# Up projection of a decoder layer in seven block products per pair of row blocks, with half-size weight slices

## Chip, cores, metric

One core of a Trainium2 chip runs the whole layer in one launch. The metric is the device time of that core in microseconds; "before" is the median of 3 runs. TensorE is called PE here, VectorE DVE, ScalarE ACT, GpSimd POOL and SyncE SP. Each engine takes its instructions strictly in the order in which the program wrote them and waits on semaphores that others raise.

## Reference, cut to what matters

```python
mix = jnp.concatenate([attn, gated], axis=-1)
h = h + mix @ w_out                                                    # 1024 x 1024
f = jnp.square(jax.nn.relu(rmsnorm(h, norm2_g) @ w_up)) @ w_down       # 1024 x 4096, 4096 x 1024
h = h + f
gate = jax.nn.sigmoid(rmsnorm(h, gate_norm_g) @ w_gate)                # 1024 x 1024
return h + gate * (p @ w_ple)                                          # then the final rmsnorm
```

There are 2080 tokens (32 of the decoder sample, 2048 of the prompt), float32 throughout. Ahead of this stand the input projection, the dilated attention and the gated mixing; none of that is touched.

## The kernel before, in words

The tail (function `finish`) keeps activations transposed, features on the partitions and tokens along the free axis, in four **groups** of 544, 512, 512 and 512 tokens (`GROUPS`). A float32 product is made of three fast matmuls: every operand is split into a rounded high half and the low remainder, and `mm3` (L1440 to L1448) issues high x high (L1443), high x low (L1444) and low x high (L1445) into one PSUM bank. A matmul's stationary operand is a 128x128 piece of weights, its moving operand up to 512 tokens; group 0 is cut into two halves of 272.

The work is a flat list of jobs J, one after another on PE. `up_job(g, f)` makes row block f of the hidden layer (32 blocks of 128): 8 contraction blocks x 3 matmuls over the tokens, then relu (L1477), square (L1478) and the high copy (L1479) on ACT and the low remainder on DVE (L1480). `down_job(g, f, 2)` takes two row blocks of the hidden layer and adds 8 output blocks, 2 x 3 matmuls each, into `acc` on DVE (L1493). A steady stretch is two up jobs and a down job: 48 + 48 matmuls of 512 columns, called a **pair** below; 16 pairs make a group. The gate jobs of group g-1 and the output projection (`out_job`) of group g+1 are put between the pairs of group g, and the second norm of group g+1 (`norm`, L1407 to L1411) is spread behind its output projection, several pairs before that group begins: `zha/zla` and `zhb/zlb` alternate, so one group's operand is written while the other is read.

Weights come as **slices** of 128x1024: a DMA into one of two raw buffers (L1269), a high copy on ACT (`S.copy`, L1287), a low remainder on POOL or, for every fourth slice, on DVE (L1288). Five slices stand in a ring (`RING = 5`). A slice is written into the queues some steps ahead of its use (`split_one`, at most one per 3 steps of PE time), or, where it has not been by then, right at its first use (`Weights.__getitem__`). Since each queue is in order, what stands ahead of the copy in ACT's queue has to be done before it.

`bg()` runs one piece of the waiting elementwise work (norms, loads, final scaling) at every yield of a job, so those pieces stand between the job's own instructions.

Of the kernel before, what the change touches and what calls it, by code (L numbers as in the profile page):

```python
# [8 lines left out]
F32 = mybir.dt.float32  # L9
F32R = mybir.dt.float32r  # L10
# [4 lines left out]
P = 128  # L15
# [22 lines left out]
WX, WY = 18, (4, 2, 1)  # L38
RING, EXTRA = 5, (9, 7, 6, 5, 4, 3)
# [8 lines left out]
def build(tc, A, stop=9):  # L48
# [12 lines left out]
    with stack:  # L61
# [23 lines left out]
        zero = cp.tile([P, P], F32, name="zero")  # L85
        V.memset(zero, 0.0)
# [1163 lines left out]
        def finish(sa, att, ape):  # L1250
            zt, acc, sq_sum, hid = {}, {}, {}, {}
            work, adds = [], []
# [5 lines left out]

            def w1(nm):
                return wk.tile([P, GM], F32, tag="w1", name=nm, bufs=3)  # L1260


            wraw, wbuf = [], []

            def wload(t, src):
                if t == 0:
                    wraw.append(ape.tile([P, 2, 1024], F32, tag="kh0", name="wraw"))
                raw = wraw[0][:, t % 2]
                nc.sync.dma_start(raw if len(src.shape) == 2 else raw.rearrange("p (a b) -> p a b", a=2), src)  # L1269


            def slot(t):
                if t not in LATE:
                    if t < RING:
                        tag = ("q10", "qd2", "kl0", "raw", "raw")[t]
                        wbuf.append(ape.tile([P, 2, 1024], F32R, tag=tag, name=f"w{t}", bufs=1 + (tag == "raw")))
                    return wbuf[ring_no(t) % RING]
                e = LATE.index(t)
                if e % 2 == 0:
                    b = wk.tile([P, KD, GM], F32R, tag=("zha", "zla", "acca")[e // 2], name=f"w{t}")  # L1280
                    b = b.rearrange("p a b -> p (a b)")[:, :4096].rearrange("p (s a b) -> p s a b", s=2, a=2)
                    wbuf[RING:] = [b[:, 0], b[:, 1]]
                return wbuf[RING + e % 2]

            def wsplit(t):
                w, raw = slot(t), wraw[0][:, t % 2]
                S.copy(w[:, 0], raw)  # L1287
                (V if t % 4 == 3 else G).tensor_sub(w[:, 1], raw, w[:, 0].bitcast(F32))  # L1288
                return w[:, 0], w[:, 1]


            rings = {}

            def ring(tag, i, n):
# [17 lines left out]
            def mix(g):  # L1312
# [9 lines left out]
                for a in range(3 if g else 0):  # L1322
                    load()
# [5 lines left out]
                for a in range(4):  # L1329
# [8 lines left out]
                    if g and a == 2:  # L1338
# [8 lines left out]
                        for _ in range(8):  # L1347
                            yield
# [465 lines left out]
```

## Time and profile before

| what | value |
|---|---|
| runs | 2918.13 us median of 3 (2916.2 to 2918.51) |
| profiled execution | 2915.15 us, span 2913.3 us, mean granted clock 0.976 |
| PE busy | 2798.0 us of the span (96%) |
| DVE, ACT, POOL busy | 1515.2, 1299.9, 1265.0 us |
| the four groups | from about 1180 us to the end |

The span is the time from the first to the last instruction; the execution's own time is 1.85 us longer. A PE that is busy is not a PE at its peak, since matmuls overlap: what one costs is read from the distance between the starts of neighbours.

### The profile page before, as it was taken

How to read it: one execution, taken by the hardware profiler on the slowest of the kernel's cores; microseconds unless marked ns; L12 is line 12 of the kernel's file. 1: busy time of each engine (PE TensorE's matmuls, PEld its weight loads, DVE VectorE, ACT ScalarE, POOL GpSimd, SP SyncE). 2: the span in 40 equal slices, each digit the busy share in tenths (PEclk: the TensorE clock that was granted, in tenths of full speed). 3: DMA queues.
4: the chain of work that ended last, by engine and by line, in shares of the span. 5: the costliest groups of instructions: out<-in, count | busy, mean ns of one | idle time of the engine just before them, and what ended most of it. 6: DMA issues, size and time to landing. Idle time of an engine off the chain costs nothing.

```text
span 2913.3 us, 42298 instructions
## 1 busy us (share of the span) xinstructions
PE 2798.0 (96%) x15712; PEld 2399.5 (82%) x15712; DVE 1515.2 (52%) x2947; ACT 1299.9 (45%) x2363; POOL 1265.0 (43%) x899
## 2 busy tenths in 40 slices
PE   8999998989998998999999999999999999999997
PEld 8877775668888798899999798888888888888887
DVE  6686246655544457644445455446534455534347
ACT  4222453347877774533334433334433434443343
POOL 2568344534768664532222423334333334433332
PEclk9999999979999999999999999999999999999999
DMA  6668675556765774232222232423233323333232
GB/s 183 205 231 297 196 236 174 150 145 194 214 199 171 228 227 157 77 101 87 88 87 94 77 132 95 163 91 101 87 123 129 131 88 101 105 110 123 98 105 72
DMA packets 218478, 413.34 MB, mean 142 GB/s; under 512 B 19552, under 2 KB 87680, under 8 KB 218272
## 3 DMA queue, kind: packets, MB, share of 16 engines
q1 hardware_dynamic: 215584, 406.45, 43.3%
q10 hardware_dynamic: 2688, 4.20, 0.4%
q8 instruction: 124, 2.03, 0.3%
q14 instruction: 82, 0.67, 0.1%
HBM read 342.61 MB, written 67.96 MB: 141 GB/s over the span
## 4 chain that ended last, share of the span: by engine, by line
PE 57%; DVE 2%; ACT 1%; issue 0%; POOL 0%; POOLq 0%; ACTq 0%; DVEq 0%
PE u L1445 8%; PE u L1443 8%; PE u L1444 8%; PE d L1443 8%; PE d L1444 8%; PE d L1445 8%; PE g L1445 2%; PE g L1444 2%; PE g L1443 2%; DVE ss L1367 1%; PE b L1443 1%; PE b L1445 1%; PE b L1444 1%; DVE zf L1407 0%; ACT sq L1362 0%
## 5 line engine op out<-in xcount | busy, mean ns | idle before, releaser
L1288 POOL TENSOR_TENSOR w<-wraw,w 128x1024 fp32r<-128x1024 f32 x228 | 558.8, 2453 | 992.4 <-ACT w L1287 950.7
L1287 ACT CAST w<-wraw 128x1024 fp32r<-128x1024 f32 x304 | 316.5, 1045 | 348.9 <-PE d L1444 258.9
L1443 PE MATMUL d<-ring,w 128*128 128x512 f32 (+2 forms) x1312 | 457.6, 349 | 0.9 <-ACT ring L1479 0.9
L1443 PE MATMUL u<-zh,w 128*128 128x512 f32 (+1 forms) x1280 | 453.2, 354 | 3.0 <-ACT sq L1362 1.8
L1493 DVE TENSOR_TENSOR acc<-acc,d 128x512 f32<-128x512 f32 (+2 forms) x640 | 360.6, 577 | 182.0 <-PE d L1445 181.2
L1444 PE MATMUL d<-ring,w 128*128 128x512 f32 (+2 forms) x1312 | 454.8, 347 | 0.3 <-DVE ring L1480 0.3
L1445 PE MATMUL d<-ring,w 128*128 128x512 f32 (+2 forms) x1312 | 454.5, 346 | 0.0
L1444 PE MATMUL u<-zl,w 128*128 128x512 f32 (+1 forms) x1280 | 449.5, 351 | 2.6 <-POOL zl L1411 1.8
L1445 PE MATMUL u<-zh,w 128*128 128x512 f32 (+1 forms) x1280 | 451.5, 353 | 0.0
L1480 DVE TENSOR_TENSOR ring<-r,ring 128x512 fp32r<-128x512 f32 (+1 forms) x160 | 113.2, 708 | 533.3 <-ACT ring L1479 533.3
L1443 PEld LDWEIGHTS d<-ring,w 128*128 128x128 f32 x1312 | 247.7, 189 | 32.8 <-ACT ring L1479 1.1
L1445 PEld LDWEIGHTS d<-ring,w 128*128 128x128 f32 x1312 | 246.9, 188 | 33.1
L1444 PEld LDWEIGHTS u<-zl,w 128*128 128x128 f32 x1280 | 241.9, 189 | 38.0 <-POOL zl L1411 2.3
L1444 PEld LDWEIGHTS d<-ring,w 128*128 128x128 f32 x1312 | 247.3, 188 | 31.3 <-DVE ring L1480 0.5
L1443 PEld LDWEIGHTS u<-zh,w 128*128 128x128 f32 x1280 | 241.5, 189 | 37.1 <-ACT sq L1362 2.0
L1445 PEld LDWEIGHTS u<-zh,w 128*128 128x128 f32 x1280 | 241.6, 189 | 32.7
L1477 ACT ACTIVATE r<-u 128x512 f32<-128x512 f32 (+1 forms) x160 | 82.6, 516 | 287.3 <-PE u L1445 287.3
L1136 POOL TENSOR_TENSOR fl<-fr,fh 128x512 fp32r<-128x512 f32 (+1 forms) x120 | 128.4, 1075 | 134.2 <-ACT fh L1135 112.9
L306 PE MATMUL f<-xh,wh 128*128 128x512 f32 (+1 forms) x480 | 174.5, 363 | 11.2 <-ACT wh L173 5.6
L958 DVE CUSTOM_DVE_ANT_0 sm<-s,mask 128x256 f32<-128x256 f32 (+1 forms) x384 | 122.3, 363 | 108.5 <-ACT pe L968 38.0
L307 PE MATMUL f<-xl,wh 128*128 128x512 f32 (+1 forms) x480 | 172.1, 359 | 2.4 <-DVE xl L203 2.3
L308 PE MATMUL f<-xh,wl 128*128 128x512 f32 (+1 forms) x480 | 172.3, 359 | 0.4 <-DVE wl L174 0.4
(279 smaller groups left out, 5699.0 us busy)
## 6 DMA issues: line engine op xcount, KB each, us to landing
wraw<-w_up SPq DMA_DIRECT2D x128, 512.0 KB
wraw<-w_down SPq DMA_DIRECT2D x128, 512.0 KB
xr<-xT SPq DMA_DIRECT2D x72, 256.0 KB
sr<-cache_v SPq DMA_DIRECT2D x32, 512.0 KB
wraw<-w_gate SPq DMA_DIRECT2D x32, 512.0 KB
fr<-g_d SPq DMA_DIRECT2D x24, 512.0 KB
wr<-w_in SPq DMA_DIRECT2D x40, 256.0 KB
o_d<-stg SPq DMA_DIRECT2D x32, 264.0 KB
```

The source lines that it names most:

```text
L306: T.matmul(p, wh[:, k, ws], h[:, o:o + w], start=st, stop=False)
L307: T.matmul(p, wh[:, k, ws], l[:, o:o + w], start=False, stop=False)
L308: T.matmul(p, wl[:, k, ws], h[:, o:o + w], start=False, stop=sp)
L958: V.tensor_tensor_reduce(sm[:, c], sp[:, c], mask[:, 256 * d + (256 - P * nk if d < 2 else 0):256 * d + (256 if d < 2 else P)], scale=1.0, ...
L1136: G.tensor_sub(l, raw, h.bitcast(F32))
L1287: S.copy(w[:, 0], raw)
L1288: (V if t % 4 == 3 else G).tensor_sub(w[:, 1], raw, w[:, 0].bitcast(F32))
L1443: T.matmul(p, wh, zh, start=(x == 0), stop=False)
L1444: T.matmul(p, wh, zl, start=False, stop=False)
L1445: T.matmul(p, wl, zh, start=False, stop=(x == n - 1))
L1480: V.tensor_sub(hl[:, c], r, hh[:, c].bitcast(F32))
L1493: V.tensor_add(acc[g][:, d, c], acc[g][:, d, c], p)
```

## The change

For two row blocks of the up projection (f, f+1), the two halves of the contraction (4 of 8 blocks each) and the two halves of the tokens, the 2x2 block product is made from **seven** block products instead of eight (Winograd's form of Strassen's scheme). A product is 4 contraction blocks x 3 matmuls over half a group's tokens (256 or 272): 84 matmuls per pair where there were 48 of 512 columns (96 of 272 in group 0). Around them:

- The weight operands are half slices of 128x512. Three of the seven are halves of the weights, four are sums or differences, made on POOL (L1807) ahead of the split. Every up slice's low half is made on POOL, and of the others two in three. `RING = 8` half slices; six raw places instead of two whole ones.
- The token operands are seven blocks in high and low form (`zc`), one buffer for all groups, made by `blocks(g)`: per contraction block two scalings, four subtractions and two of the low remainders on DVE, four high copies on ACT and two remainders on POOL. `blocks(g+1)` stands behind group g's last up job, between its last two down jobs.
- The products are put together by seven DVE additions of half a group (L1583 to L1597) and one ACT copy (L1581); relu, square, copy and low remainder then run per row block.
- Gate jobs work on half a group, so gate weights are read and split twice per group.

```diff
-RING, EXTRA = 5, (9, 7, 6, 5, 4, 3)
+RING = 8
...
             def up_job(g, f):
                 def run(ws):
...
+                    def prod(x, y):
+                        w = ws[x]
+                        p = ps7[x] = bank(f"u{g}_{f}_{x}", m)
+                        for k in range(4):
+                            kk = slice(P * k, P * k + P)
+                            T.matmul(p, w[0][:, kk], zh[y][:, k, :], start=(k == 0), stop=False)
+                            T.matmul(p, w[0][:, kk], zl[y][:, k, :], start=False, stop=False)
+                            T.matmul(p, w[1][:, kk], zh[y][:, k, :], start=False, stop=(k == 3))
+                            steps[0] += 3 * m / 2400
+                            if k == 1:
+                                yield
+                        use(1)
+                        yield
...
+                    yield from prod(0, 5)
+                    yield from prod(1, 3)
+                    yield from prod(2, 0)
+                    S.copy(U1, ps7[2])
+                    yield from prod(3, 6)
+                    V.tensor_add(U2, U1, ps7[3])
+                    yield from prod(4, 4)
+                    V.tensor_add(U3, U2, ps7[4])
+                    V.tensor_add(U2, U2, ps7[1])
+                    r, t = two(f"r{g}_{f}")
+                    V.tensor_add(r[1], U3, ps7[1])
+                    V.tensor_add(r[0], U3, ps7[0])
+                    for x, c in [(t, slice(0, n))] if t is not None else zip(r, cs):
+                        S.activation(x, x, AF.Relu)
+                        hidden(x, 1, c)
+                    yield from prod(5, 1)
+                    r, t = two(f"q{g}_{f}")
+                    V.tensor_add(r[0], U1, ps7[5])
+                    yield from prod(6, 2)
+                    V.tensor_add(r[1], U2, ps7[6])
+                    for x, c in [(t, slice(0, n))] if t is not None else zip(r, cs):
+                        S.activation(x, x, AF.Relu)
+                        hidden(x, 0, c)
...
+            def make_low():
+                t = low[0]
+                h, o, e, end = sl[t]
+                w = got[t]
+                (G if o or end is False or t % 3 else V).tensor_sub(w[:, 1], place(h), w[:, 0].bitcast(F32))
...
+            def make():
+                if low[0] is not None:
+                    make_low()
+                if not can_make():
+                    return
...
+                if o:
+                    G.tensor_tensor(place(h), place(o[0]), place(o[1]), op=o[2])
+                w = got[t] = slot(t)
+                S.copy(w[:, 0], place(h))
...
+                    t = made[0]
+                    if steps[0] >= last_made[0] + 1.4:
+                        if low[0] is not None or (can_make() and steps[0] >= born[sl[t][0]] + 4):
+                            make()
```

Three places of the built program show how the queues move. First, ACT's queue over one steady pair of group 1. L1809 is the high copy of a weight slice (L1287 before), L1591 and L1599 the relus of the two row blocks, L1567 and L1568 their square and copy, L1581 the copy of product 2. Before, row blocks 24 and 25:

```order
L1477 ACTIVATE r1_24_0_18654<-u1_24_0_18627 128x512
L1478 ACTIVATE r1_24_0_18654<-r1_24_0_18654 128x512
L1479 CAST ring0_12135<-r1_24_0_18654 128x512
L1287 CAST w0_11289<-wraw_11197 128x1024
L1477 ACTIVATE r1_25_0_18687<-u1_25_0_18659 128x512
L1478 ACTIVATE r1_25_0_18687<-r1_25_0_18687 128x512
L1479 CAST ring0_12135<-r1_25_0_18687 128x512
```

and of the change, row blocks 24 and 25 as one pair:

```order
L1581 COPY ring3_12065<-u1_24_2_19939 128x256
L1809 CAST w4_11596<-wraw_11195 128x512
L1591 ACTIVATE r1_24_19988<-r1_24_19988 128x512
L1567 ACTIVATE r1_24_19988<-r1_24_19988 128x512
L1568 CAST ring0_12062<-r1_24_19988 128x512
L1809 CAST w6_11664<-wraw_11195 128x512 x2
L1599 ACTIVATE q1_24_20012<-q1_24_20012 128x512
L1567 ACTIVATE q1_24_20012<-q1_24_20012 128x512
L1568 CAST ring0_12062<-q1_24_20012 128x512
L1809 CAST w0_11289<-wraw_11195 128x512
L1809 CAST w0_11289<-wraw2_11530 128x512
```

The weight copies among the relus were those of up 26 and 27, whose turn on PE comes after the next down job. Now the two copies behind the first relu chain are those of product 6 of this same pair and of the coming down job's first row block (both go to ring tile w6), and the down job's second slice stands behind the second relu chain.

Second, PE over the same stretch, with the semaphores waited for. Before, where up 24 ends and up 25 begins (w2 is its slice, zh21 and zl21 the token operand):

```order
L1444 MATMUL u1_24_0_18627<-zl21_12404,w1_11361 128x512
L1445 MATMUL u1_24_0_18627<-zh21_12403,w1_11361 128x512
L1443 MATMUL u1_25_0_18659<-zh21_12403,w2_11611 128x512 [waits DVE_49,Activation_49]
L1444 MATMUL u1_25_0_18659<-zl21_12404,w2_11611 128x512
L1445 MATMUL u1_25_0_18659<-zh21_12403,w2_11611 128x512
```

and of the change, where product 5 ends and product 6 begins, and where the down job begins (w6 and w0 are ring tiles of two slices each, ring0 to ring2 the hidden layer's high and low parts):

```order
L1559 MATMUL u1_24_5_19998<-zc_first_11505,w4_11596 128x256
L1557 MATMUL u1_24_6_20016<-zc_first_11505,w6_11664 128x256 [waits Activation_49]
L1558 MATMUL u1_24_6_20016<-zc_first_11505,w6_11664 128x256
L1559 MATMUL u1_24_6_20016<-zc_first_11505,w6_11664 128x256 [waits Pool_49]
...
L1517 MATMUL d1_22_0_0_20039<-ring1_12063,w6_11664 128x512 [waits DVE_49,Activation_49]
L1518 MATMUL d1_22_0_0_20039<-ring2_12064,w6_11664 128x512
L1519 MATMUL d1_22_0_0_20039<-ring1_12063,w6_11664 128x512 [waits Pool_49]
L1517 MATMUL d1_22_0_0_20039<-ring0_12062,w0_11289 128x512 [waits Activation_49]
L1518 MATMUL d1_22_0_0_20039<-ring1_12063,w0_11289 128x512
L1519 MATMUL d1_22_0_0_20039<-ring0_12062,w0_11289 128x512 [waits DVE_49]
```

Before, the wait for a slice stands at the head of a job of 24 matmuls. Now product 6 waits at its first matmul for the high half (Activation) and at its third for the low half (Pool), and the down job's two slices are waited for in the same way at its first, third, fourth and sixth matmul.

Third, POOL around the step from group 1 to group 2. Before, the low remainders of the second norm (L1411) among weight slices, behind the twelfth pair of group 1:

```order
L1288 TENSOR_TENSOR w1_11361<-wraw_11197,w1_11361 128x1024
L1288 TENSOR_TENSOR w2_11611<-wraw_11197,w2_11611 128x1024
L1411 TENSOR_TENSOR zl22_19127<-zf22_0_0_19128,zh22_19126 128x512
L1411 TENSOR_TENSOR zl22_19127<-zf22_2_0_19157,zh22_19126 128x512
L1411 TENSOR_TENSOR zl22_19127<-zf22_4_0_19183,zh22_19126 128x512
L1288 TENSOR_TENSOR w4_11782<-wraw_11197,w4_11782 128x1024
L1411 TENSOR_TENSOR zl22_19127<-zf22_6_0_19210,zh22_19126 128x512
L1288 TENSOR_TENSOR w0_11289<-wraw_11197,w0_11289 128x1024
```

and of the change, between the last two down jobs of group 1 (L1439 is the low remainder of a token block, L1782 that of a weight slice):

```order
L1782 TENSOR_TENSOR w0_11289<-wraw2_11530,w0_11289 128x512 x2
L1439 TENSOR_TENSOR zc_first_11505<-wraw2_11530,zc_first_11505 128x2x256
L1439 TENSOR_TENSOR zc_first_11505<-w1b_11531,zc_first_11505 128x2x256
L1439 TENSOR_TENSOR zc_first_11505<-ring3_12065,zc_first_11505 128x2x256 x2
L1439 TENSOR_TENSOR zc_first_11505<-wraw2_11530,zc_first_11505 128x2x256
L1439 TENSOR_TENSOR zc_first_11505<-w1b_11531,zc_first_11505 128x2x256
L1439 TENSOR_TENSOR zc_first_11505<-ring3_12065,zc_first_11505 128x2x256 x2
L1782 TENSOR_TENSOR w2_11480<-wraw_11195,w2_11480 128x512
L1782 TENSOR_TENSOR w4_11596<-wraw_11195,w4_11596 128x512
```

All eight token remainders now stand in one run, behind the first two or three slices of the last-but-one down job and ahead of its fourth (the L1782 row on w2) and of everything the last down job needs.

## Rows read from the trace of the kernel before

**Rows 1.** The page's busy line: busy us, share of span, xinstructions.

```profile
PE 2798.0 (96%) x15712; PEld 2399.5 (82%) x15712; DVE 1515.2 (52%) x2947; ACT 1299.9 (45%) x2363; POOL 1265.0 (43%) x899
```

**Rows 2.** The page's chain that ended last, share of the span by engine.

```profile
PE 57%; DVE 2%; ACT 1%; issue 0%; POOL 0%; POOLq 0%; ACTq 0%; DVEq 0%
```

**Rows 3.** A stage of group 2: busy us by engine, clock, DMA.

```profile
core 0: us, PE busy (x) PEld busy (x) DVE busy (x) ACT busy (x) POOL busy (x), PEclk, DMA share, GB/s
2030.00:2430.00 400.00, 400.00 (x1742) 325.02 (x1742) 192.66 (x248) 156.88 (x223) 146.45 (x64) 1.00 0.34 112
```

**Rows 4.** Waits: waiter, awaited, total us, times, longest.

```profile
POOL w L1288 <- ACT w L1287: 950.7, 198, 12.3
ACT w L1287 <- PE d L1444: 258.9, 41, 9.3
```

**Rows 5.** Timeline of PE: start us, us; pieces of 512, 272, 256 columns.

```profile
2000.09 0.40 PE L1443 MATMUL d<-ring,w 128*128 128x512 f32 x1
...
2011.88 0.40 PE L1443 MATMUL u<-zh,w 128*128 128x512 f32 x1
...
1500.41 0.29 PE L1445 MATMUL u<-zh,w 128*128 128x272 f32 x1
...
1502.67 0.30 PE L1445 MATMUL u<-zh,w 128*128 128x272 f32 x1
...
2869.73 0.28 PE L1443 MATMUL g<-zh,w 128*128 128x256 f32 x1
...
2879.94 0.28 PE L1443 MATMUL g<-zh,w 128*128 128x256 f32 x1
```

**Rows 6.** Timeline: a row block's last matmul and its relu.

```profile
1501.16 0.29 PE L1445 MATMUL u<-zh,w 128*128 128x272 f32 x1
...
1501.49 0.40 ACT L1477 ACTIVATE r<-u 128x272 f32<-128x272 f32 x1 [1.70 <-PE u L1445]
```

**Rows 7.** Tile d: duration ns min/median/max, starts, forms.

```profile
L1493 DVE TENSOR_TENSOR acc<-acc,d x640: 407/676/690, 1217.5 to 2856.2; 128x512 f32<-128x512 f32 x92, 128x272 f32<-128x272 f32 x64, 128x256 f32<-128x256 f32 x4
```

**Rows 8.** Groups by line and form: xcount, busy us, mean ns.

```profile
L1493 DVE TENSOR_TENSOR acc<-acc,d 128x272 f32<-128x272 f32 x256 | 108.2, 435 | 55.1 <-PE d L1445 55.0
...
L1136 POOL TENSOR_TENSOR fl<-fr,fh 128x512 fp32r<-128x512 f32 x72 | 91.9, 1281 | 78.8 <-ACT fh L1135 66.7 <-PE o L999 6.0 <-DMA re<-o_d 4.9
...
L1478 ACT ACTIVATE r<-r 128x512 f32<-128x512 f32 x96 | 60.7, 632 | 3.1
...
L1479 ACT CAST ring<-r 128x512 fp32r<-128x512 f32 x96 | 59.6, 620 | 3.1
...
L1477 ACT ACTIVATE r<-u 128x512 f32<-128x512 f32 x96 | 57.2, 596 | 209.5 <-PE u L1445 209.5
...
L1407 DVE SCALAR_TENSOR_TENSOR zf<-acc,gains,rb 128x512 f32<-128x512 f32 x40 | 48.5, 1212 | 3.0 <-ACT rb L127 3.0
...
L1478 ACT ACTIVATE r<-r 128x272 f32<-128x272 f32 x64 | 27.6, 432 | 2.0
```

**Rows 9.** Windows of 5 us in the last stretch (columns as in rows 3).

```profile
2835.00:2840.00 5.00, 3.92 (x20) 3.95 (x21) 2.60 (x6) 2.76 (x5) 0.48 (x1) 0.66 0.34 120
```

**Rows 10.** Timeline of PE in that stretch.

```profile
2833.96 0.28 PE L1445 MATMUL d<-ring,w 128*128 128x256 f32 x1
...
2836.08 0.85 PE L97 MATMUL rc<-ones,ss 128*128 128x1 f32 x4 [1.85 <-DVE ss L1367]
...
2837.16 0.41 PE L1444 MATMUL d<-ring,w 128*128 128x256 f32 x1
...
2839.50 0.35 PE L1443 MATMUL d<-ring,w 128*128 128x256 f32 x1
```

**Rows 11.** Timeline: a DVE remainder beside POOL's, and one alone.

```profile
2017.87 2.50 POOL L1288 TENSOR_TENSOR w<-wraw,w 128x1024 fp32r<-128x1024 f32 x1 [5.97 <-ACT w L1287]
...
2019.63 1.29 DVE L1480 TENSOR_TENSOR ring<-r,ring 128x512 fp32r<-128x512 f32 x1 [1.53 <-ACT ring L1479]
...
2025.08 0.69 DVE L1480 TENSOR_TENSOR ring<-r,ring 128x512 fp32r<-128x512 f32 x1 [4.15 <-ACT ring L1479]
```

More of the change, by code (lines that the diff above doesn't have):

```diff
@@ L1272, in slot @@
-            def slot(t):
[L1273 to L1294, printed above, removed]
+                more()
+                turn[0] += 1
+                return scratch[turn[0] % 2]
+            wbuf, places, extra = [], [], []
+            def more():
+                if not extra:
+                    assert mixed
+                    t = ape.tile([P, SEQ], F32, tag="raw", name="wraw2", bufs=2)
+                    extra.extend((t[:, 0:512], t[:, 512:1024]))
+                    scratch.append(t[:, 1024:1024 + GM])
+                    scratch.append(att.tile([P, GM], F32, tag="re1", name="w1b", bufs=2))
@@ L1465, in run @@
                             yield
-                return ([A["w_out"][d:d + 2, :, 0:512].rearrange("d p f -> p d f")], run)
+                        use(1)
+                return ("rows", [A["w_out"][d + x, :, 0:512] for x in range(2)], run)
             def up_job(g, f):
@@ L1484, in down_job @@
+                    for x in range(2):
+                        hid[f + x] = hs[x]
+                w = [A["w_up"][f + x] for x in range(2)]
+                return ("pair", [w[0][:, 0:512], w[1][:, 0:512], w[0][:, 512:], w[1][:, 512:]], run)
             def down_job(g, f0, nf, last=False):
@@ L1495, in run @@
                                     square("3", g, d, c)
+                            if d % 4 == 3 and (g < 3 or not last or cs[0].start):
+                                use(nf)
                             yield
                         if last and g == 3:
-                            work.append(norm("3", g, cs[0]))
-                return ([A["w_down"][f0 + x] for x in range(nf)], run)
+                            work.append(norm3(g, cs[0]))
+                return ("rows", [A["w_down"][f0 + x, :, 512 * y:512 * y + 512] for y in range(2) for x in range(nf)], run)
             gates, pws = [], {}
@@ L1547, in run @@
                         work.append(final(3, c))
-                return ([A["w_gate"][d] for d in range(d0, d0 + nd) if c.start == 0], run)
+                return ("rows", [h for d in range(d0, d0 + nd) if c.start == 0 for h in w_gate(d)], run)
             def bg():
```

359 lines of the change are left out of this document (239 added, 120 removed).

## Prediction

> **What bounds the kernel now.** I read the page's busy line first: PE is busy for 96% of the span [rows 1]. The chain of waits is mostly PE too, 57%, with 2% DVE and 1% ACT [rows 2]. The stage windows say where: in 400 us of group 2 PE shows no gap at all, at a granted clock of 1.00 (2.4 GHz), while DVE, ACT and POOL are busy for 193, 157 and 146 us [rows 3]. The waits say how the weights are kept out of the way: POOL waits 950.7 us for ACT's high copies, and ACT waits 258.9 us for a down job to give back a ring slot [rows 4]. So the split runs ahead until the ring is full, and PE meets finished slices. The reader is to see that a gain must come out of PE's matmuls, and that it is lost as soon as PE meets a slice that isn't finished.
>
> What a matmul costs is the distance of starts: 51 from 2000.09 to 2011.88 us, 0.2312 us each at 512 columns; 18 from 1500.41 to 1502.67, 0.1256 at 272; 87 from 2869.73 to 2879.94, 0.1174 at 256 [rows 5]. Halving the columns costs 1.5% more per column, no more.
>
> **What is removed.** A pair was 48 x 0.2312 = 11.10 us and is 84 x 0.1174 = 9.86: 1.24 us less, in 48 pairs 59.5. In group 0, 96 x 0.1256 against 84 x 0.1256: 1.51 less, in 16 pairs 24.1. The gates of groups 1 and 2 in halves cost 16 x (48 x 0.1174 - 24 x 0.2312) = 1.4. Together **-82 us**, if PE never waits.
>
> **What is added on PE's path.** The order rows show that it will wait. In every pair the high copy for product 6 stands in ACT's queue behind the relu chain of the first row block, and that chain needs product 4. Meanwhile PE has product 5 to do, 12 x 0.1174 = 1.41 us. From the end of product 4's issue:
> - 0.20 until the consumer starts: relu starts 0.33 after the start of the last matmul [rows 6], of which one spacing lies before that end;
> - four dependent DVE additions of half a group out of PSUM, 0.41 each, the shortest of that kind [rows 7], 1.64;
> - relu, square, copy of 512 columns, 0.60 + 0.63 + 0.62 [rows 8], 1.85;
> - the high copy of a half slice, a cast of 128x512, 0.62 [rows 8].
>
> That is 4.31, and PE is idle for 4.31 - 1.41 = 2.90. The third matmul needs the low half, a POOL subtraction of 128x512, 1.28 [rows 8]; two matmuls cover 0.23, idle 1.05. Then the down job: its second slice is copied behind the second relu chain, which needs product 6. That takes 0.20 + 0.41 + 1.85 + 0.62 = 3.08; three matmuls of the first slice cover 0.69, idle 2.39. Its low half: 1.28 - 0.46 = 0.82. Per pair 2.90 + 1.05 + 2.39 + 0.82 = 7.16, in 48 pairs 344.
>
> In group 0 the additions take 0.435 and each chain runs for two halves of 272, six operations of about 0.43 [rows 8]: 0.20 + 1.74 + 2.58 + 0.62 - 1.51 = 3.63; 1.28 - 0.25 = 1.03; 0.20 + 0.44 + 2.58 + 0.62 - 0.38 = 3.46; 1.03. Sum 9.15, in 16 pairs 146. Together **+490**. Nothing can hide these four waits: PE's queue is in order and everything ahead of them is used up. Below, they can only shrink if the chain's operations are shorter than such rows; above, POOL's may be longer.
>
> **The clock.** After 2 us without matmuls (2833.96 to 2836.08) the spacing at 256 columns is 0.213 (11 from 2837.16 to 2839.50) instead of 0.117, and the granted clock of those 5 us is 0.66: the lower level, 1.2 GHz, for part of them [rows 9, 10]. The change has two gaps of that length in each pair. At half clock the ten matmuls of product 6 behind its wait cost 10 x 0.096 = 0.96 more, and behind the second gap I take again the 2.9 us of wide spacing seen there, of which half, 1.45, is loss. The waits hide the rest. 2.4 x 64 pairs = **+154**; the bounds are 0 (no fall) and 3.5 per pair, 224.
>
> **Gates.** Four gate jobs stand together twelve times. The first slice of the pair behind them is copied behind the fourth gate's sigmoid and a square, 0.20 + 0.43 + 0.43 + 0.62 = 1.68 after it. From there POOL makes the pair's slices in turn, with nothing ahead: eight operations (low halves of 0 to 4, three sums) of 1.28 and three copies of 0.62 between them, 12.1, and ten last matmuls, 1.17. That makes 14.95 to the end of product 4, where five products take 7.05; with 0.9 for the low half of the third gate's first slice, 8.8 each: **+106**. Bounds: 40 if POOL finds its operands earlier than the order shows, 150.
>
> **Group steps.** The next group's operand was made many pairs ahead; now `blocks` runs between the last two down jobs, on DVE, for which PE waits. A step is two scalings of 1.21 [rows 8], low remainders of 0.41 and 0.69 [rows 7, 11] and four subtractions of 0.41: 5.2. Counted from the end of product 6: chain and remainder 3.15, first step to 8.3, ACT's casts and the second slice's copy to 9.55, low half 10.8, first addition to `acc` 11.9; then three steps with two additions of 0.68 and a remainder of 0.69 between, to 29.4; cast 0.62, remainder 1.28, and only then, on POOL, the down job's fourth slice, 1.28: 32.6. In a steady pair the same matmul comes at 9.9. So 22.7; 6 more for the next group's first two pairs, whose slices are again made in turn: 29 x 3 = **+87**, bounds 40 and 120. The first group's blocks and the norm casts ahead of six pairs' copies add about **+28** (10 + 6 x 3), bounds 0 and 60.
>
> DMA I cost at nothing: six raw places of 256 KB, eight loads in a pair of some 28 us, at a DMA share of 0.34 [rows 3]; if they came late, ACT's copies would be late next. Matmuls that no longer run leave nothing else behind.
>
> **A rule against the change.** In one place DVE's remainder of 512 columns takes 1.29 us while POOL's subtraction runs, and 0.69 alone [rows 11]. The Trainium skill, SBUF — State Buffer, Who interferes with whom, says that DVE and GpSimd share one port pair as an exclusive lock. The trace agrees here. Per pair two of POOL's operations lie on the path, each next to a DVE remainder; if each had to sit one out, 2 x 0.69 x 64 = 88 us come on top. I leave them out of the sum, because the remainder starts at least as early as the copy that POOL waits for and is all but over by then.
>
> **Sum.** -82 + 490 + 154 + 106 + 87 + 28 = +783. The profiled execution was 2915.15 with a span of 2913.3, so 3698; the median of the runs is 3 above it: **3700 us**.
>
> **Rivals.**
> - *The clock holds.* Then nothing runs at the lower level between the waits. For it: group 2's clock of 1.00 [rows 3], and that PE still works for two thirds of a pair. Against it: a gap of 2 us was enough in the last stretch, and these are 2.4 and 2.9 [rows 9, 10]. 3700 - 154 = 3546. Chance 0.2.
> - *DVE and POOL exclude each other* on the path, as above: 3788. Chance 0.14.
> - *Gates and group steps are half hidden*, since POOL and DVE catch up while PE waits elsewhere: 3700 - 97 = 3603. Chance 0.1.
> - *The slices are ready*: ACT runs a pair ahead after all, so that the relu chains hold up nothing. Then the four waits, the clock, the gates' queue and the group steps vanish, 2918 - 82 + 28 = 2864. It decides at 82 / 64 = 1.28 us of waiting per pair against the 7.16 counted; against it speaks every order row. Chance 0.04, of which 0.01 for no change.
> - My own case: 0.52, 3620 to 3780 by itself.
>
> The range is 3520 to 3820: it holds the first three rivals and leaves out the last, and the case in which all upper bounds come together. A measurement of this kernel can tell about 0.2% from no change. Faster 0.03, same 0.01, slower 0.96.
>
> **What would show it.** In the new profile PE's busy share in the groups should fall to 70 or 75%, with a granted clock near 0.85 there. Product 6's first matmul (L1557) should be idle for about 2.9 us on L1809's copy in every pair, its third on L1782, the down job's fourth (L1517) 2.4 us on L1809 again. The starts of neighbouring pairs should be 30 to 31 us apart in groups 1 to 3 (22.2 before). If they are 21, the step "behind the relu chain" is wrong and so is the forecast; if they are 28, the clock held.

## The result and the profile after

The change takes 3819.4 us (median of four runs, 3816.4 to 3823.3) where the kernel before takes 2917.2: ratio 1.310, 95% interval 1.308 to 1.312. Slower was forecast; 902 us were lost where 783 had been counted. That is the very top of the range: its upper end, 3820, lies 902 us above the 2918.1 from which the forecast started. The busy line and the chain of the page after [rows 1, 2]:

```profile
PE 3102.8 (81%) x17632; PEld 2665.8 (70%) x17632; DVE 1755.2 (46%) x3612; ACT 1518.3 (40%) x3059; POOL 1995.8 (52%) x1673
PE 34%; POOL 23%; issue 22%; DVE 8%; ACT 7%; DMA 5%; SPq 1%; POOLq 0%; ACTq 0%; DVEq 0%
```

PE has fallen from 57 to 34% of the chain, and POOL, which had none of it, has 23. A stage of group 2 after [rows 3], and the waits that matter [rows 4]:

```profile
2350.00:2750.00 400.00, 293.18 (x1511) 243.99 (x1509) 163.01 (x271) 139.28 (x264) 209.88 (x164) 0.85 0.21 64
POOL w L1782 <- ACT w L1809: 1095.1, 419, 14.6
ACT w L1809 <- POOL wraw L1807: 490.1, 176, 4.8
PE u L1557 <- ACT w L1809: 231.5, 114, 3.8
PE u L1559 <- POOL w L1782: 124.6, 150, 3.6
PE d L1519 <- DVE w L1782: 101.1, 45, 7.8
PE d L1517 <- ACT w L1809: 76.1, 35, 7.6
ACT w L1809 <- DMA wraw<-w_up: 125.9, 39, 7.0
```

PE's busy share is 73% and the clock 0.85, as foretold. ACT and POOL wait for each other, and PE for both; the waits for DVE's low halves and for DMA were in no term of mine. A pair of group 1, first PE, then ACT and POOL:

```profile
2216.14 0.28 PE L1559 MATMUL u<-zc_first,w 128*128 128x256 f32 x1
2219.13 0.58 PE L1557 MATMUL u<-zc_first,w 128*128 128x256 f32 x1 [2.71 <-ACT w L1809]
...
2220.48 0.58 PE L1559 MATMUL u<-zc_first,w 128*128 128x256 f32 x1 [0.55 <-POOL w L1782]
...
2223.64 0.63 PE L1519 MATMUL d<-ring,w 128*128 128x512 f32 x1
2225.99 0.80 PE L1517 MATMUL d<-ring,w 128*128 128x512 f32 x1 [1.73 <-ACT w L1809]
```

```profile
2216.62 0.63 ACT L1591 ACTIVATE r<-r 128x512 f32<-128x512 f32 x1 [3.67 <-DVE r L1589]
2217.28 0.63 ACT L1567 ACTIVATE r<-r 128x512 f32<-128x512 f32 x1
2217.94 0.62 ACT L1568 CAST ring<-r 128x512 fp32r<-128x512 f32 x1
2218.47 1.13 ACT L1809 CAST w<-wraw 128x512 fp32r<-128x512 f32 x2
...
2219.16 2.50 POOL L1782 TENSOR_TENSOR w<-wraw,w 128x512 fp32r<-128x512 f32 x2 [3.15 <-ACT w L1809]
```

The copy that product 6 needs starts at 2218.47, behind relu, square and copy. Plain pairs of groups 1 to 3, those with no gates, norm or group step near them, are 30.5 to 30.7 us apart from end to end of their up jobs, but every third is 33.8 to 34.3.

**Lost time.** For the comparison I took all 11,328 matmuls of the token part (what follows the attention), subtracted from each distance of starts the spacing that its columns have [rows 5], and summed the rest by job. After, 1050 us are lost, before 66. The difference of 984, less the 82 that the columns give, is 902; the spans differ by 908, of which 6 us arise ahead of this part. In the table a down job just ahead of a group step counts whole under group steps.

| lost time, us | forecast | after | pace 1.2 | no sums |
|---|---|---|---|---|
| product 6 and down jobs: four waits and clock | 490 + 154 | 629 | 216 | 637 |
| gate jobs and the up jobs behind them | 106 | 159 | 62 | 120 |
| group steps | 87 | 131 | 52 | 118 |
| first blocks, casts, out jobs' pairs, other up products | 28 | 68 | 100 | 33 |
| the rest (norm's sums, out jobs, last gates) | as before, 66 | 63 | 129 | 60 |

### The profile page after: what moved, and what is told of

Read it like the earlier page. It is cut to its first block, busy times and chain, and to the rows that moved or that the text cites. A ratio compares the mean times of both kernels' runs of the same rounds, so it can differ in the third digit from the quotient of the medians.

```text
span 3821.5 us, 49746 instructions
## 1 busy us (share of the span) xinstructions
PE 3102.8 (81%) x17632; PEld 2665.8 (70%) x17632; DVE 1755.2 (46%) x3612; ACT 1518.3 (40%) x3059; POOL 1995.8 (52%) x1673
## 4 chain that ended last, share of the span: by engine, by line
PE 34%; POOL 23%; issue 22%; DVE 8%; ACT 7%; DMA 5%; SPq 1%; POOLq 0%; ACTq 0%; DVEq 0%
POOL w L1782 13%; POOL wraw L1807 7%; PE d L1519 4%; PE d L1517 3%; PE d L1518 3%; DMA wraw<-w_up 3%; PE o L996 2%; PE f L303 2%; PE f L305 2%; PE f L304 2%; PE u L1559 1%; PE t L307 1%; PE t L308 1%; PE t L309 1%; DVE w L1782 1%
## 5 line engine op out<-in xcount | busy, mean ns | idle before, releaser
L1782 POOL TENSOR_TENSOR w<-wraw,w 128x512 fp32r<-128x512 f32 x708 | 923.7, 1318 | 1148.5 <-ACT w L1809 1095.1
L1557 PE MATMUL u<-zc_first,w 128*128 128x256 f32 (+1 forms) x1792 | 566.9, 316 | 245.0 <-ACT w L1809 231.5
L1809 ACT CAST w<-wraw 128x512 fp32r<-128x512 f32 x834 | 485.7, 615 | 675.1 <-POOL wraw L1807 490.1
L1559 PE MATMUL u<-zc_first,w 128*128 128x256 f32 (+1 forms) x1792 | 576.6, 322 | 124.9 <-POOL w L1782 124.6
L1519 PE MATMUL d<-ring,w 128*128 128x512 f32 (+2 forms) x1312 | 522.4, 398 | 137.0 <-DVE w L1782 101.1
L1517 PE MATMUL d<-ring,w 128*128 128x512 f32 (+2 forms) x1312 | 529.4, 403 | 76.3 <-ACT w L1809 76.1
L1557 PEld LDWEIGHTS u<-zc_first,w 128*128 128x128 f32 x1792 | 383.3, 214 | 273.5 <-ACT w L1809 257.8
L1616 DVE TENSOR_TENSOR acc<-acc,d 128x512 f32<-128x512 f32 (+2 forms) x640 | 369.6, 580 | 436.9 <-PE d L1519 435.7
L1558 PE MATMUL u<-zc_first,w 128*128 128x256 f32 (+1 forms) x1792 | 551.5, 308 | 5.3 <-POOL zc_first L1439 5.3
L1518 PE MATMUL d<-ring,w 128*128 128x512 f32 (+2 forms) x1312 | 511.8, 390 | 0.0
L1559 PEld LDWEIGHTS u<-zc_first,w 128*128 128x128 f32 x1792 | 386.1, 215 | 161.8 <-POOL w L1782 161.6
L1519 PEld LDWEIGHTS d<-ring,w 128*128 128x128 f32 x1312 | 287.8, 219 | 217.5 <-DVE w L1782 127.2
L1558 PEld LDWEIGHTS u<-zc_first,w 128*128 128x128 f32 x1792 | 385.9, 215 | 7.5 <-POOL zc_first L1439 6.1
L1517 PEld LDWEIGHTS d<-ring,w 128*128 128x128 f32 x1312 | 294.4, 224 | 135.4 <-ACT w L1809 100.4
L1518 PEld LDWEIGHTS d<-ring,w 128*128 128x128 f32 x1312 | 292.5, 223 | 38.8 <-issue 3.6
L1807 POOL TENSOR_TENSOR wraw<-wraw 128x512 f32<-128x512 f32 x178 | 235.5, 1323 | 2.0
L1583 DVE TENSOR_TENSOR ring<-ring,u 128x256 f32<-128x256 f32 (+1 forms) x64 | 27.2, 426 | 382.0 <-PE u L1559 306.9
```

What stands on the lines that cost most here:

```text
L1517: T.matmul(p, wh, zh, start=(x == 0), stop=False)
L1518: T.matmul(p, wh, zl, start=False, stop=False)
L1519: T.matmul(p, wl, zh, start=False, stop=(x == n - 1))
L1557: T.matmul(p, w[0][:, kk], zh[y][:, k, :], start=(k == 0), stop=False)
L1558: T.matmul(p, w[0][:, kk], zl[y][:, k, :], start=False, stop=False)
L1559: T.matmul(p, w[1][:, kk], zh[y][:, k, :], start=False, stop=(k == 3))
```

## The experiments

Each was timed in rounds with the kernel before, four runs each.

**Undo the stall alone: the pace.**

```diff
-                    if steps[0] >= last_made[0] + 1.4:
+                    if steps[0] >= last_made[0] + 1.2:
```

> One number: a slice may be made 1.2 steps after the last one, not 1.4. The up job yields every 0.64 steps and the down job every 1.28, so that 1.4 becomes 1.92 and 2.56 in effect and the job ends with its last slices made on demand; with 1.2 the order shows the copies of products 5, 6 and of the down job's first two slices a whole job ahead of the relu chains. Theory A (the waits behind the relu chains, as forecast): the four waits of a pair vanish with the clock loss that follows them, 9.5 us in each of 64 pairs, and part of the 13 us at each of 12 places of gate jobs; 3819 becomes 2950 to 3150, a plain pair of groups 1 to 3 is 21 to 23 us, not 30.5, and PE's waits on L1809 for product 6 are gone. Rival B (POOL and DVE are the limit, and the relu chain only shows where it ends last): a pair needs about 13.7 operations of 1.28 on POOL, 17.5 us, and where DVE shuts POOL out more; then a plain pair is 25 to 28 us and the time 3250 to 3500, with PE waiting for L1782.

3326 us, ratio 1.141 (1.138 to 1.143): 493 less by one number. The four waits are gone from their places, and others stand there. In group 1, first product 4 at its first and third matmul, then product 6; below, ACT and DVE at product 6:

```profile
2075.59 0.39 PE L1557 MATMUL u<-zc_first,w 128*128 128x256 f32 x1 [0.45 <-ACT w L1809]
2076.93 0.39 PE L1559 MATMUL u<-zc_first,w 128*128 128x256 f32 x1 [0.85 <-POOL w L1782]
2081.40 0.38 PE L1557 MATMUL u<-zc_first,w 128*128 128x256 f32 x1 [1.60 <-ACT ring L1581]
```

```profile
2080.98 0.36 ACT L1581 COPY ring<-u 128x256 f32<-128x256 f32 x1
2081.38 0.42 DVE L1583 TENSOR_TENSOR ring<-ring,u 128x256 f32<-128x256 f32 x1 [11.92 <-ACT ring L1581]
```

Product 6 no longer waits for a slice but for the copy of product 2 out of PSUM (L1581), which stands in ACT's queue behind weight copies: it starts 0.06 us after that copy's end, when the first of the additions (L1583) has only begun. Products 3 and 4 wait for slices. So theory A is right about the place: the waits behind the relu chains, 413 of the first row's 629 us, go with the pace. The time and the distance of plain pairs, 24.8 to 28.9 us in groups 1 to 3, are rival B's: behind the relu chains a second limit was hidden. What it is, the early sums below show.

**The clock.** Matmuls whose result nobody reads, in the waits:

```diff
+                        if x == 5:
+                            keep_busy(ps7[2], w, zh[y][:, 0, :], 20)
...
+                                    keep_busy(free[0][0], w[0], free[0][1], 8)
```

> Added are 36 matmuls per pair whose results nobody reads, on operands that are there already: 20 of half a group ahead of product 6, 8 ahead of the third and 8 ahead of the fourth matmul of the down job; they take 2.35, 0.94 and 0.94 us in waits of 2.9, about 1.1 and 2.0. Theory A (the granted clock falls because PE stands still): the spacing behind the waits stays at 0.117 and 0.231, the granted clock of groups 1 to 3 goes from 0.84 to 0.95 or more, and the time falls by 120 to 230, the slow spacings of all pairs being worth 231 us in the trace. Rival B (the clock's cost is hidden by the next wait, since a product that is done sooner only waits longer): the clock rises but the time falls by less than 60. Rival C (the lower level has another cause): clock and time stay as they are, or the time grows by some us where a wait is shorter than what fills it.

3718 us, ratio 1.275 (1.271 to 1.278): 101 less. The same two windows, first after, then with the fillers (the clock is the third number from the end):

```profile
1200.00:1600.00 400.00, 311.93 (x2031) 296.13 (x2032) 153.76 (x333) 139.27 (x292) 216.21 (x167) 0.83 0.20 61
2250.00:2650.00 400.00, 303.57 (x1525) 251.52 (x1525) 158.44 (x264) 136.31 (x253) 207.73 (x162) 0.84 0.21 64
```

```profile
1200.00:1600.00 400.00, 356.09 (x2656) 344.08 (x2657) 161.80 (x356) 149.97 (x315) 230.01 (x179) 0.96 0.21 67
2250.00:2650.00 400.00, 320.07 (x1887) 276.30 (x1887) 169.77 (x282) 142.82 (x270) 210.87 (x166) 0.93 0.21 68
```

The wide spacings sum to 233 us after and to 110 with fillers: 123 us of them gone, 101 of time won. Here the lower level (1.2 GHz) goes with PE's standing still: with the waits filled the clock of these windows rises from 0.83 and 0.84 to 0.96 and 0.93. It costs nearly its face value. The time falls between A and B.

**POOL's chain.** The sums of half slices left out:

```diff
-                    G.tensor_tensor(place(h), place(o[0]), place(o[1]), op=o[2])
+                    pass
```

> Left out are the four sums of half slices on POOL per pair (L1807): products 1, 3, 4 and 6 take the raw half slice in their place, so the output differs. Theory A (POOL's serial chain costs only where slices are made on demand one after the other, behind gates, out jobs and group steps): plain pairs stay at 30.5 us; the up job behind four gate jobs, 16 us over its columns' time now, loses three sums of 1.3, so 12 x 4 = 48, and the first two pairs of three groups about 4 each, 24, with 10 more behind out jobs: 70 to 100 less, 3720 to 3750. Rival B (POOL is the limit in every pair): 4 x 1.3 x 64 = 333 less, about 3490. Rival C (the gates' waits are ACT's queue, not POOL): no change.

3726 us, ratio 1.279 (1.275 to 1.282): 93 less, theory A. The last column above: pairs' own loss unchanged, gates 39, steps 13, casts and other up products 35 less.

**The third pairs.** In every third pair the first slice of the down job has its low half on DVE, and the third matmul waits for it. After, PE and DVE at such a place:

```profile
2747.88 0.53 PE L1518 MATMUL d<-ring,w 128*128 128x512 f32 x1
2752.55 0.79 PE L1519 MATMUL d<-ring,w 128*128 128x512 f32 x1 [4.15 <-DVE w L1782]
```

```profile
2750.12 0.69 DVE L1569 TENSOR_TENSOR ring<-q,ring 128x512 fp32r<-128x512 f32 x1 [2.01 <-ACT ring L1568]
2750.73 1.77 DVE L1782 TENSOR_TENSOR w<-wraw,w 128x512 fp32r<-128x512 f32 x1
```

DVE's queue holds the low half behind the remainder of the second relu chain. (Where it is the second slice's that falls on DVE, in another third of the pairs, the down job loses no more than elsewhere.) The edit puts the low halves of all down slices on POOL:

```diff
+                    sl += [(i + x, None, [], 2 if kind == "down" else True) for x in range(len(srcs))]
...
-                (G if o or end is False or t % 3 else V).tensor_sub(...)
+                (G if o or end is False or end == 2 or t % 3 else V).tensor_sub(...)
```

> The low halves of the down jobs' slices are all made on POOL; before, every third slice's is made on DVE (t % 3). Theory A, formed on the trace after: where this falls on the first or second slice of a down job, the DVE subtraction stands behind the remainder of the second relu chain, and the down job loses 8.0 us over its columns' time, not 4.6; that is so in about every third pair, some 20 of 64, and was not in my forecast, which took POOL for all of them. Then the time falls by 20 x 3.4 = 68, to about 3750, and the down jobs' cycle of 4.6, 4.8, 8.0 becomes even. Rival B (the third pairs lose it to something else, such as their place in the ring of raw half slices, which has six): no change. Rival C (POOL's longer queue costs as much as it gives): within 20 us.

3788 us, ratio 1.299 (1.297 to 1.301): 32 less. The down jobs' lost time, 4.6, 4.8, 8.0 in turn, becomes 5.1, 5.2, 5.1: the place is as theory A says, but the other two thirds of the pairs lose 0.4 to 0.5 us more each, presumably to POOL's longer queue, so that only half of the 68 comes.

**Slower matmuls behind gates and steps.**

```diff
+                        if 0 < x < 5 and g and f in (0, 2, 10, 12, 16, 18):
+                            for _ in range(8):
+                                T.matmul(p, zh[y][:, 0, 0:P], zh[y][:, 0, :], start=True, stop=True)
```

> The changed kernel (pace 1.4), and ahead of products 1 to 4 of the pairs behind gate jobs and of the first two pairs of groups 1 to 3, 18 up jobs in all, eight matmuls of half a group whose results nobody reads, on operands of that group. They take 0.94 us each time, in waits of 0.5 to 1.4. My term for the clock counted slow spacing only behind the two gaps of a pair; the trace shows 233 us of it against 154, of which 158 lie in product 6 and in the down jobs and 35 + 24 behind gates and steps. Theory A (the lower level there costs time): 20 to 60 less, 3760 to 3800. Rival B (POOL's chain sets the end of these up jobs, PE's speed between the waits doesn't count): within 15 of 3819, with the slow spacings gone and the waits longer. Rival C: the fillers are longer than the waits: up to 30 more.

3817 us, ratio 1.308 (1.306 to 1.311), no change. The fillers took away 19 of the 59 us of wide spacing there, no more, so it is a weak test; the time is within B's bound, and what was taken away gave nothing.

**The norm's remainders.**

```diff
-                        (G if k % 2 else V).tensor_sub(zl[:, k - 1, :], ...)
+                        V.tensor_sub(zl[:, k - 1, :], ...)
```

> The changed kernel (pace 1.4) with the low halves of the gates' operand (norm3, L1485) all on DVE, where four of eight in each half were on POOL among the slices. Theory A (behind gate jobs POOL doesn't make the slices "with nothing ahead", as I put it: remainders of the norm stand between them): the up jobs behind the fourth to eighth gate, 18 us over their columns' time against 14 where no norm piece follows, and the pairs ahead of which a norm is made, lose 2 to 4 us each; 15 to 45 less in all. Rival B (DVE's own work beside POOL stretches both, so that it doesn't matter which has the remainder): within 10 of 3819.

3806 us, ratio 1.304 (1.302 to 1.307): 13 less, between the theories. The worst up jobs behind gates (the fifth to eighth gate of groups 1 and 2) lose 16.4, not 18.1. But there are three such places, others lose up to 1 us more, and the table's row of gates falls only from 159 to 157; most of the gain stands in the first row, 629 to 619. So the remainders on POOL cost something behind those gates, but not much of what was missing. What POOL does after, in a pair with norm pieces that is not behind gates:

```profile
2548.53 0.93 POOL L1485 TENSOR_TENSOR zx_first<-w1b,zx_first 128x256 fp32r<-128x256 f32 x1
2549.41 1.57 POOL L1782 TENSOR_TENSOR w<-wraw,w 128x512 fp32r<-128x512 f32 x1
```

**The group step.** The next group's operand is not made; the diff takes the line with `blocks(g + 1)` out.

> Left out is the making of the operand of the up projection for groups 1 to 3 (blocks): their products read what group 0 left, so the output differs. Theory A (a group step is two things: DVE's blocks ahead of the down job's additions, and behind it two pairs whose slices POOL makes in turn): the down job of row blocks 28 and 29 goes from 30 us over its columns' time to about 5, 3 x 25 = 75 less, and the next two up jobs keep their 11 us each; 3730 to 3760. Rival B (those two up jobs too are late by the blocks): 3 x 12 more, 3690 to 3720. Rival C (without blocks the step waits for the slices as long): within 20 of 3819.

3741 us, ratio 1.282 (1.280 to 1.284): 79 less, theory A. The down job ahead of the step loses 5.6, 5.1 and 4.9 us in the three groups, not 29.7, 30.0 and 30.1, and the two up jobs behind it keep what they lost (11 us each in groups 2 and 3, 14 and 12 in group 1).

**The ring without the seven products.** `up_job` and `blocks` are replaced by plain row blocks:

```diff
+                    for x in range(2):
+                        w = [ws[2 * x + y] for y in range(2)]
...
+                        use(2)
...
+                return ("rows", [w[0][:, 0:512], w[0][:, 512:], w[1][:, 0:512], w[1][:, 512:]], run)
```

> One part of the change alone: weights in half slices through the ring of eight, six raw places, the pace of 1.4 and the operand of the next group made between the last two down jobs, but the up projection as before, row block by row block with eight block rows of operands, 96 matmuls of 512 columns in a pair and down job, no sums and no additions of products: 8 slices per pair instead of 11. In ACT's queue the down job's second slice still stands behind the relu chain of the second row block in a pair, and the last slice of the second row block behind the first one's chain. Theory A (the loss comes from ring and pace together with the chains, and seven products make it worse because they need 11 slices): one wait of about 2 and its low half's 0.8 stay in each pair, some clock, group steps of 20: 64 x 3.5 + 60 to 100, 3180 to 3300. Rival B (the seven products alone cause it; eight slices come in time): 2950 to 3030. Rival C (ring and pace cause nearly all): over 3500.

3017 us, ratio 1.034 (1.033 to 1.036): theory B. My own count of a wait in each pair was wrong here; the lost time of the whole token part is 169 us. With yields 1.28 steps apart in the down job a pace of 1.4 comes to one slice in 2.56, four per job; here the up job, with yields 2.56 apart, makes the other four of eight. An up job of seven products (yields 0.64 apart, a slice in 1.92) makes 4.7, so 8.7 in a pair that needs eleven; the last ones are then made on demand. With the pace of 1.2 a slice is due at every second yield of the up job and at each of the down job, 7 + 8 = 15.

**Building on the pace.** Sums ahead of the low half that stood before them:

```diff
+                if job[0] == "pair":
+                    early.update({x + 1: [x + 1, x + 4], x + 2: [x + 3], x + 4: [x + 6]})
```

> The pace of 1.2 as in the first experiment (3326), and POOL makes each sum of half slices ahead of the low half that stood before it, where its operands allow: sum 4 goes right behind sum 1, sum 3 ahead of low half 2, sum 6 ahead of low half 4. With the pace alone POOL stood still for 0.73 us at each copy that needed a sum, four times in a pair, and ACT stood 2.6 to 3.4 us at each sum with everything else in its queue behind. Theory A (what is left with the pace of 1.2 is this taking of turns between ACT and POOL): the waits for slices 3 and 4, 58 us in plain pairs and some 40 behind gates and steps, go, and product 6's, 80 us, which waits for additions whose first operand ACT copies behind such a copy, shrinks by half; 3326 becomes 3180 to 3250. Rival B (POOL and DVE stretch each other, so that POOL's work itself is the bound): less than 40 is won.

3210 us, ratio 1.100 (1.098 to 1.102): 116 less than with the pace alone, theory A. Then the additions:

```diff
-                    S.copy(U1, ps7[2])
+                    V.tensor_copy(U1, ps7[2])
...
+                    V.tensor_add(r[0], U3, ps7[0])
                     V.tensor_add(U2, U2, ps7[1])
                     V.tensor_add(r[1], U3, ps7[1])
-                    V.tensor_add(r[0], U3, ps7[0])
```

> As the run with early sums, and in the chain of the first row block two more edits: the copy of product 2 out of PSUM is made by DVE, not in ACT's queue, and the addition that gives product 0's bank back comes second, not fourth (product 6 is the seventh product and there are six banks, so its first matmul waits for that addition too). Theory A (with slices ready, the chain of additions is the next wait for product 6): product 6's first wait, 80 us with the pace alone, goes to under 15; 40 to 80 less than the run with early sums. Rival B (product 6 waits for its slice then): within 20 of it.

3191 us, ratio 1.094 (1.092 to 1.096): 19 less. The number is B's, but the reason is neither theory's. Product 6 does not wait for the addition on product 0, as the first experiment's rows show, and it does not wait for its slice here:

```profile
PE u L1557 <- DVE ring L1581: 19.2, 9, 2.6
```

It waits for the copy of product 2 still, now on DVE. By the distance of starts that wait was 80 us with the pace alone, 29 with the early sums and 21 here: the early sums had already taken most of it. Here is a stretch of two pairs of group 2 in this kernel:

```profile
2511.00:2553.00 42.00, 40.33 (x248) 35.68 (x247) 20.95 (x37) 21.72 (x38) 35.79 (x28) 1.00 0.35 113
```

Two neighbouring up jobs in it end at 2520.9 and 2542.0, a pair of 21.1 us against 22.2 before. Between these two ends PE is never idle. The columns' gain exists there, at a clock of 1.00, with POOL busy for 85% of the stretch.

Two other pacings: first a due time (`due[0] = max(due[0], steps[0] - 1) + 1.5`), which spreads the slices evenly but gives less lead (one in 1.5 steps, where the pace of 1.2 comes to one in 1.28), then more lead by a pace of 0.6:

> As the run before in this call, with another pacing: a due time that grows by 1.5 steps per slice, not 1.2 after the last one, so that slices are also made between the two relu chains of a pair. Theory A (POOL, loaded with 17.5 us in pairs of some 21, must be kept at work evenly): 20 to 80 less than the run before. Rival B (the ring of eight half slices sets when a slice is made, the pace no longer matters): within 20.

3245 us, ratio 1.112 (1.109 to 1.114): 53 more, neither theory. Product 6 loses 7 us, not 33, but the gates and the up jobs behind them lose 101 for 56 and the down jobs 198 for 135: less lead costs where slices are short.

> The best so far (pace 1.2, sums early, additions reordered: 3191), with the pace at 0.6, so that the ring of eight alone limits how far ahead slices are made, and the norms' matmuls issued six yields later after their sums of squares (lag 12 for 6, and 3 for 2 further on), since PE waits for those sums for 89 us against 42 before. Theory A (lead is what counts: the due time of 1.5 gave less lead and cost 53 us): 40 to 110 less, 3080 to 3150. Rival B (POOL's work, with DVE beside it, is the bound now): within 30 of 3191.

3241 us, ratio 1.111 (1.109 to 1.113): 50 more, neither theory. Two of the expected gains came (norm 89 to 62, the table's row of other up products 75 to 26), but the down jobs' lost time rose from 135 to 229:

```profile
PEld d L1517 <- DVE acc L1616: 121.2, 40, 5.9
PE d L1517 <- DVE acc L1616: 110.6, 38, 5.4
```

PE waits there for additions that give PSUM banks back (76 and 68 us without the two edits). What the pace did by itself, without the later norm matmuls, no run shows.

**The start of POOL's chain behind gates.** Squares on DVE:

```diff
-                    if key == "f" and g == 3:
+                    if key == "f":
                         V.tensor_mul(sq, acc[g][:, d, c], acc[g][:, d, c])
```

> The changed kernel (pace 1.4), with the squares behind the gates of groups 0 to 2 made by DVE (a product of acc with itself) as those of group 3 are, not by ACT. In the trace after, the first slice copy behind the fourth gate starts 2.25 us after the end of the gate's last matmul, not 1.06 as I forecast: ACT's square, which stands ahead of it, waits for two DVE operations behind the sigmoid that I left out. Theory A (that is part of what the gates cost beyond the forecast): the copy starts about 1.7 us earlier at each of 12 places and the second gates' slices too, 15 to 35 less than 3819. Rival B (the copy waits for something else, or POOL's chain isn't earlier for it): within 10.

3828 us, ratio 1.313 (1.311 to 1.315), no gain, as in B: theory A fell. What ACT and DVE do at four gates, in this kernel:

```profile
2781.03 0.38 ACT L1647 ACTIVATE sg<-g 128x256 f32<-128x256 f32 x1 [2.34 <-PE g L1519]
2782.41 0.62 ACT L1809 CAST w<-wraw 128x512 fp32r<-128x512 f32 x1 [1.00 <-DMA wraw<-w_up]
```

```profile
2774.85 1.36 DVE L1381 TENSOR_TENSOR ring<-acc 128x256 f32<-128x256 f32 x1
2776.14 0.68 DVE L1782 TENSOR_TENSOR w<-wraw,w 128x512 fp32r<-128x512 f32 x1
```

The copy now waits for its load, and the third gate for a low half that stands behind DVE's square. The up jobs at some places lose 2 us less, the gate jobs 17 us more.

**The three waits that were left**, together, on the kernel with the additions: the norms' matmuls six yields later, low halves of down jobs on POOL, squares on DVE.

> The best so far (pace 1.2, sums early, additions reordered: 3191) with three edits: the norms' matmuls six yields later (this alone took their waits from 89 to 62 us in the run with the pace of 0.6), the low halves of the down jobs' slices all on POOL, so that DVE's additions, which give PSUM banks back, don't stand behind them (PE waits 144 us for these additions), and the gates' squares on DVE. Theory A (three separate waits, all on PE's path): 25 + 15 to 40 + 10, 3110 to 3150. Rival B (POOL, with 20 more operations, is the bound and gives it back): 3180 to 3230. In neither case does it reach the kernel before, 2917.

3160 us, ratio 1.083 (1.081 to 1.086): 31 less, between A and B. Still lost are 391 us; 66 + 82 = 148 would be level with the kernel before. No version with seven products reaches it, and the ring without them, at 3017, does not either.

## Why the forecast was right in kind and 119 us short

The mechanism was right: the four waits stand where they were forecast, for the reason given, and cost what was counted. What was short lies in the terms for slices made on demand.

- **Columns, -82:** right. The spacings hold, and a pair without waits shows the gain.
- **Four waits, +490, and the clock, +154:** 629 together against 644. In the pair shown PE stood 2.99 us at product 6's first matmul from start to start, 2.87 more than a spacing, against 2.90; the down job's fourth came 2.35 behind its third, 2.12 more than a spacing, against 2.39. That the place in the queue is the cause is shown by the pace, which alone takes 413 of the 629 away. Missing was the third pairs' wait for DVE, worth 32 net; it is inside the 629, made up by chains somewhat shorter than counted, so that the sum's closeness is in that part luck.
- **"Nothing can hide these four waits"** holds for the order as built. That order is a matter of the pace, though: ACT was 40% busy.
- **The step that failed is the stretch in which slices are made on demand, "POOL makes the pair's slices in turn, with nothing ahead": its terms were too small.** Gates measured 159 for 106, group steps 131 for 87, the rest 68 for 28; that is +137, of which the pairs' own -15 and the 63 for 66 of the last row take 18 back, which leaves the 119. (Of the 131, 14 are the three down jobs' ordinary waits, which the forecast has among the four waits; by its own count the steps measured 117 and the pairs 643 for 644.) POOL's chain itself was right: after, the eight operations run from 2782.45 to about 2794.8, 12.3 us for 12.1. PE, ACT and POOL there:

```profile
2779.41 0.28 PE L1519 MATMUL g<-zx_first,w 128*128 128x256 f32 x1
2782.43 0.58 PE L1557 MATMUL u<-zc_first,w 128*128 128x256 f32 x1 [2.74 <-ACT w L1809]
```

```profile
2779.72 0.38 ACT L1647 ACTIVATE sg<-g 128x256 f32<-128x256 f32 x1 [0.25 <-PE g L1519]
2781.45 0.42 ACT L1383 ACTIVATE ring<-acc 128x256 f32<-128x256 f32 x1 [1.35 <-DVE ssf L1388]
2781.78 0.60 ACT L1809 CAST w<-wraw 128x512 fp32r<-128x512 f32 x1
```

```profile
2782.45 1.27 POOL L1782 TENSOR_TENSOR w<-wraw,w 128x512 fp32r<-128x512 f32 x1 [4.43 <-ACT w L1809]
...
2793.52 2.51 POOL L1782 TENSOR_TENSOR w<-wraw,w 128x512 fp32r<-128x512 f32 x2 [0.73 <-ACT w L1809]
```

What it was short of stands around the chain. The last gate's last matmul starts at 2779.41 and is issued by 2779.53, and the copy starts 2.25 us later, not 1.06: the square (L1383) waits for DVE operations behind the sigmoid. The gates' own slices cost 2.0 a place, not 0.9. At six of the twelve places gates and up job lose 11 us together, where 8.8 were counted; at the other six, where pieces of a norm or of the final scaling stand among the slices, 14 to 17. So most of the missing 53 us arise at the second kind, and the cause there stays open: putting the norm's remainders on DVE took only 2 us from the row of gates, and taking the square away moved the wait to DVE and to a load. The 53 us are placed, not attributed to one cause.
- **Group steps:** the down job was right (25.4 for 22.7); the next two up jobs together lose 13.4 beyond a plain pair's two, for 6 counted. Without blocks they lose the same, so the blocks are not the cause; that it is their slices, made in turn, fits the 13 us that the steps lose less without the sums.
- **DMA at nothing:** not quite. ACT waited 126 us for up weights after, mostly while PE worked in a down job; the run with the squares moved shows a load next in line behind gates.
- **Rivals.** The clock does not hold (0.84). Gates and steps are not half hidden. The time that comes nearest, 3788, belongs to DVE and POOL excluding each other on the path, but its 88 us would stand in the first row, which has 629 for 644, and POOL's operations on the path are not longer (the two behind product 6's copy take 1.25 each in the pair above, 1.28 having been counted). Elsewhere DVE and POOL do stretch each other, 1.77 for 0.69 above, 1.57 for 1.27; moving work between them gave 32 and 13 us. The Trainium skill, SBUF — State Buffer, Who interferes with whom, says that a DVE operation with two SBUF inputs contends with a GpSimd instruction that reads SBUF; these rows agree in kind. "The slices are ready" was made true by the pace for product 6 and the down job, and even then was not a gain: the second limit showed.

## What to carry over

A product that needs fewer columns but more prepared operands (eleven slices for eight) is priced by what prepares them: first count slices per pair against what the pacing rule makes in the program's own yields. Where an in-order queue serves both, put the operand copy ahead of the chain that waits for the product. After one wait is removed, look at the next limit in the same place before counting the gain, and count what stands around a chain on demand (the operation ahead of its first copy, the pieces among its links), not the chain alone.

## What was not expected

Both other pacings cost time: less lead, evenly spread, 53 us; more lead 50 us, net of what the norm gained in the same run, with PE's waits moved to PSUM banks held by DVE's additions. And PE's slower clock, once the waits of the pairs were filled, gave back 101 of 123 us of wide spacing, while 19 us less of it behind gates and steps gave nothing. That POOL's chain sets the end there would explain it, but was not shown by itself.
